# Attention with deferred value products: four key blocks at a time, and row maxima over two PSUM banks

## The chip, the cores and the metric

The kernel runs on one core of one Trainium2 chip, in one launch. The metric is the device time of that launch in microseconds (us). A core has a matrix engine (PE, with weight loads shown apart as PEld), a vector engine (DVE), an activation engine (ACT), a general engine (POOL) and a queue of transfers (SP). [...]

## The reference

One decoder layer on 4096 tokens of width 1024: RMSNorm, one input projection, three token mixers (a gated MLP over chunks, a gated linear recurrence, and attention with a forget bias), one output projection, residual and a final RMSNorm. Only the attention is touched. It has 8 heads of 64 channels and is causal:

```python
c = jnp.cumsum(jnp.transpose(log_f, (0, 2, 1)), axis=-1)
for blk in range(seq // C_BLOCK):                       # 128 queries
    s = einsum('bhqd,bhkd->bhqk', qh[q0:q1], kh[:q1]) * scale
    s = s + c[q0:q1, None] - c[None, :q1]
    s = where(mask, s, -inf)
    p = softmax(s, axis=-1)
    o = einsum('bhqk,bhkd->bhqd', p, vh[:q1])
```

## The kernel before, in words

Phase 1 (projection and the two other mixers, with the operands of attention written to DRAM) lasts until about 1661 us of the profiled span, attention from about 1674 to 3159 us, the output projection from there to the end.

Attention works on *units*: a pair of heads `p` (four of them) and a block `Q` of 512 queries (eight), 32 units in all. It has two passes.

- The row-max pass (`rowmax`, `rm_product`) forms scores with queries on the partitions: one product `sm` of 128 queries by 512 keys (line L128), whose maximum over the keys DVE finds with one instruction (`mp<-sm`, L137). Where the keys reach past the queries (the last 512 keys of a unit, "diagonal"), L132 adds the mask and takes the maximum, with a second small instruction that reads the result. `rm_tail` gathers a unit's maxima, transposes them on PE (`mt`, L1166) and they become an extra row of the query operand.
- The second pass takes one *step* for each block of 128 keys, 4(Q+1) in a unit, 576 in all. In a step each of the two heads has two accumulating products with keys on the partitions (`st`, L1353 and L1356), then ACT takes the exponential into a tile `pt` (L1360). `do_pv` multiplies `pt` by the values (`pv`, L1238; plain float32, 64 columns wide, one head on either half of the array, and so two instructions each on PE), and adds `pt` into a running sum: DVE for head 0, POOL for head 1 (`acc`, L1247). A step's `do_pv` is issued in the next step, behind the first of that step's two row-max products. On the diagonal POOL zeroes the weights of later keys (L1365) and the widths shrink to 384, 256 and 128.
- `finish_unit` is a generator advanced once a step by `tick(fin)`: it loads the gate, multiplies the sums by ones on PE to get the denominators (`pl`, L1206), takes their reciprocal by Ln and Exp on ACT (L1210, L1211) with a Newton step on DVE and POOL (L1213 to L1216), and scales `pv` (L1218).

The order of PE's instructions is the order of the code. On DVE, ACT and POOL the framework sets a fixed order when it builds the program. The row-max pass runs ahead by `LEAD` = 76 products, 38 steps; so the last 38 steps have no `sm`. PSUM in attention: two banks for `st` (pool `ps_st`), four for the tag `sm` (pool `ps_sm`: `sm`, `mt`, `pl`, and the output projection's `o`), two for `pv`. Tiles of a pool are given out in turn, and the next user of a buffer waits for the last reader of the one before.

Of the kernel before, what the change touches and what calls it, by code (L numbers as in the profile page):

```python
# [21 lines left out]
P = 128  # L22
# [11 lines left out]
def tile_trunk(  # L34
# [42 lines left out]
    # units of attention whose row maxima are found before the last projections  # L77
# [13 lines left out]
    def rsqrt_small(pool, ssum, n, scale, tag, y=None):  # L91
        """[P, n] sums -> 1/sqrt(sum * scale + EPS), full float32 accuracy."""
# [29 lines left out]

    def rm_product(ps, qb, kb, hi_, diag, tri, dst):
        """scores of 128 queries and 512 keys of one head, and their row maxima"""
# [13 lines left out]

    def rm_rows(p, Q, mp, mm, m2):
        """row maxima over all key groups, less the offset: high and low parts, negated"""  # L140
# [16 lines left out]
    # =====================================================================  # L157
    # Phase 1: RMSNorm, input projection, gMLP, HGRN2, FoX operands
    # =====================================================================
    with ExitStack() as p1:  # L160
# [68 lines left out]
        def xnorm(i0, n):  # L229
            """generator: reciprocal RMS of n token tiles from i0."""  # L230
# [8 lines left out]
        def xprep(T, own_norm=False):  # L239
            """generator: hT[T] = (hi, lo), [P, KC, 256] each."""  # L240
# [43 lines left out]
        def setup_gen():  # L284
            # gMLP
# [23 lines left out]
            # keep source position s (partition) <= target position t  # L309
# [7 lines left out]
            # softmax over the single layer, cumulative sum less its first row  # L317
# [17 lines left out]
            # mixing is linear: LayerNorm's gain goes after it, and its offset  # L335
            # becomes off[t, c] = ln_b[c] * sum_s w[t, s] + b_s[t]
# [6 lines left out]
            # masks of the levels inside a block of 32: [source s, targets in second halves]  # L343
# [7 lines left out]
            for li, h in enumerate(levels[2:]):  # L351
# [4 lines left out]
                # s - 2h*n >= 0  # L356
# [4 lines left out]
                # 2h*n + h - 1 - s >= 0  # L361
# [9 lines left out]
            # head selector columns  # L371
# [5 lines left out]
            # carried state, block-diagonal over the two heads of a tile  # L377
# [4 lines left out]
            # scores: zero for good where the source is in a later block than the target  # L382
# [13 lines left out]
        def hgrn(T):  # L396
            """generator for 256 tokens (two chunks), after its inputs are on chip."""
            z, qf, v = Zb.pop(T), Qf.pop(T), Vb[T]
            lb, oml = setup["lb"], setup["oml"]
            # sigmoid(z) = exp(-L), sigmoid(-z) = exp(-(z + L)), L = ln(1 + exp(-z))  # L400
# [28 lines left out]
            for st in range(len(levels) + 4):  # L429
                if st == 1:  # L430
                    dq = sm.tile([P, 8], F32, tag="dq", name="dq")
                    nc.vector.tensor_copy(dq, pd.rearrange("p c n -> p (c n)"))
                    sc = hg_state["sc"][0]  # r, (chunk, a), t
                    hg_state["sc"].rotate(-1)
                    # blocks of 32 on the diagonal, side by side
                    s32 = wk.tile([P, 8, 32], F32, tag="s32", name="s32", bufs=1)  # (chunk, a, r), t
# [6 lines left out]
                # take over the level scores  # L443
# [24 lines left out]
                # q / k times decay to the middle of each block  # L468
                li = st
                if 0 <= li < 7:  # L470
# [14 lines left out]
                    else:  # L485
                        # both heads' targets side by side, each over zeros in the other's rows
# [12 lines left out]
                if st == 7:  # L499
                    # carry terms  # L500
# [29 lines left out]
                # level products: the two heads of a tile go to different banks  # L530
# [87 lines left out]
            # RMS norm over the value channels  # L618
# [14 lines left out]
        def cgen(B):  # L633
# [12 lines left out]
            # log1p(e) = ln(u) + (e - (u - 1)) / u  # L646
# [43 lines left out]
            # reference offsets of each 512-query group, on all partitions  # L690
# [24 lines left out]
        def silu(ps, dst, scale=1.0):  # L715
            """dst = scale * silu(ps), scale a power of two; dst holds scale * ps meanwhile."""
# [7 lines left out]
        def gelu(ps, dst):  # L724
            """dst = gelu(ps), the tanh form written as x * sigmoid(2 y)."""
# [48 lines left out]
        def y_store(T, yt, row0, gain=1.0):  # L774
            """transpose token-major [P, 2, 256] and store at feature rows row0.."""
# [244 lines left out]
        for gi, (B, g) in enumerate(seq):  # L1020
# [6 lines left out]
            for ti in range(BT):  # L1027
# [10 lines left out]
                # next weights  # L1038
# [7 lines left out]
                # side work  # L1046
# [24 lines left out]
    # =====================================================================  # L1071
    # Phase 2: forgetting attention
    # =====================================================================
    nc.scalar.preload_act_table_set(LN_EXP_SET)
    with ExitStack() as p2:
        fs = p2.enter_context(tc.tile_pool(name="fs", bufs=3))
        ac = p2.enter_context(tc.tile_pool(name="ac", bufs=2))
        pp = p2.enter_context(tc.tile_pool(name="pp", bufs=7))
# [3 lines left out]
        ps_sm = p2.enter_context(tc.tile_pool(name="ps_sm", bufs=4, space=PSUM))  # L1082
# [22 lines left out]
        def load_ka(i):  # L1105
            """[k hi; k lo] and the values of 512 keys, two heads."""
# [21 lines left out]
        def rowmax():  # L1128
            """generator: each step is one score product of the row-max pass."""
            tails = []  # L1130
            for u, (p, Q) in list(enumerate(units))[U0:]:
# [5 lines left out]
                for cj in range(Q + 1):  # L1137
                    for hi_ in range(8):
                        ps = ps_sm.tile([P, 512], F32, tag="sm", name="sm")
                        rm_product(  # L1140
                            ps, qb, kb_t[p * NJ + cj], hi_, cj == Q, tri, mp[:, hi_, cj : cj + 1]
                        )
# [15 lines left out]
        def rm_tail(u, mp):  # L1158
# [4 lines left out]
            for _ in range(3 if u == 0 else 6):  # L1163
                yield
# [6 lines left out]
        def unit_load(u):  # L1171
            """query side of the second pass; the row maxima go below the low parts."""
# [23 lines left out]
        def finish_unit(u):  # L1196
            """generator: normalise, gate and store one unit's output."""
# [14 lines left out]
            # one Newton step: r (2 - l r)  # L1212
# [15 lines left out]
        def do_pv(u, kb, pts):  # L1228
            p, Q = units[u]
            nkb = 4 * (Q + 1)  # L1230
            q0, _ = q0_of(u, kb)
            if kb == 0:
# [97 lines left out]
        for si, (u, kb) in enumerate(steps):  # L1330
# [40 lines left out]
            if pend is not None:  # L1371
                do_pv(*pend)
# [119 lines left out]
```

## Time and profile before

| what | value |
|---|---|
| median of three timed runs | 3522.6 us (3509.25, 3522.6, 3523.05) |
| profiled execution, first to last instruction | 3516.6 us |
| attention in it | about 1674 to 3159 us |
| mean granted PE clock | 0.982 |
| busy: PE, DVE, ACT, POOL | 97%, 71%, 45%, 40% |

For the profiled execution the page gives its span alone, no time of its own; the span is 6.0 us below the median of the timed runs. In timeline rows the first number is the start and the second the duration in us, and xN merges N instructions that follow one another, their duration being that of the whole run. The end of a matrix product is modelled: successive products overlap, so that the distance between starts tells the rate. In rows of groups the numbers behind the count are total busy us and mean ns of one, then the engine's idle time ahead of them and what ended it. In rows of windows each engine's busy us stand with the number of instructions in brackets, then the granted clock (1.00 is full), the DMA share and GB/s.

### The profile page before, as it was taken

Reading aid. Unit: us, or ns where it says so; the run is one execution under the profiler, and the core shown is the slowest. Engines: PE = TensorE matmul, PEld = TensorE weight load, DVE = VectorE, ACT = ScalarE, POOL = GpSimd, SP = SyncE. Lnnn points to the kernel's source line nnn. Section 1 sums busy time; section 2 is a strip of 40 time slices with the busy share of each in tenths; the row PEclk is TensorE's granted clock in tenths of the full one; section 3 lists DMA queues with packets and bytes.
Section 4 is the critical chain, followed back from the end, with each engine's and each line's share of the span. In section 5 each row is a group of like instructions: output and inputs, shape, how many; then the busy total and the mean of one; then the engine's idle time right before and its main releaser. Section 6 shows DMA issues by size and latency. Waiting matters only on the chain.

```text
span 3516.6 us, 63564 instructions
## 1 busy us (share of the span) xinstructions
PE 3417.2 (97%) x24375; PEld 2569.8 (73%) x24375; DVE 2482.6 (71%) x5111; ACT 1584.4 (45%) x2883; POOL 1422.0 (40%) x1468
## 2 busy tenths in 40 slices
PE   7999999999999999988999999999999999999999
PEld 7999999999999998988444444444444444448887
DVE  6467746685467756782798878888889888965554
ACT  6335544356435543452345445454544554562221
POOL 2134422333134322352465466555665666570000
PEclk9999999999999999999799899999999999999999
DMA  5332333214332223212731141014101321013442
GB/s 178 109 94 64 97 127 116 79 53 159 97 104 68 70 85 111 67 49 78 155 77 34 49 118 43 19 41 120 55 28 28 97 64 37 28 64 135 148 146 96
DMA packets 227603, 297.75 MB, mean 85 GB/s; under 512 B 19602, under 2 KB 172448, under 8 KB 227298
## 3 DMA queue, kind: packets, MB, share of 16 engines
q1 hardware_dynamic: 227298, 293.69, 27.7%
q8 instruction: 191, 3.13, 0.4%
q14 instruction: 114, 0.93, 0.1%
HBM read 208.96 MB, written 84.43 MB: 83 GB/s over the span
## 4 chain that ended last, share of the span: by engine, by line
PE 76%; DVE 13%; ACT 4%; POOL 3%; issue 2%; DMA 2%; SPq 0%; DVEq 0%; POOLq 0%; ACTq 0%
PE acc L885 15%; PE pv L1238 13%; PE acc L906 12%; PE o L1430 10%; PE sm L128 9%; PE st L1353 7%; PE st L1356 6%; DVE wlo L211 2%; DVE acc L1247 1%; DMA x<-in_x_dram 1%; DVE mp L137 1%; PE pl L1206 1%; DVE gt L729 1%; DVE xq L494 1%; PE plb L557 1%
## 5 line engine op out<-in xcount | busy, mean ns | idle before, releaser
L1360 ACT ACTIVATE pt<-st,bias 128x512 f32<-128x512 f32 (+3 forms) x1152 | 692.0, 648 | 711.3 <-PE st L1356 699.3
L1247 POOL TENSOR_TENSOR acc<-acc,pt 128x512 f32<-128x512 f32 (+3 forms) x544 | 700.4, 1288 | 479.9 <-ACT pt L1360 469.4
L137 DVE TENSOR_REDUCE mp<-sm 128x1 f32<-128x512 f32 x896 | 590.1, 682 | 100.1 <-PE sm L128 92.3
L1238 PE MATMUL pv<-pt,v 128*64 128x512 f32 (+3 forms) x2304 | 587.7, 589 | 7.2 <-POOL pt L1365 4.5
L885 PE MATMUL acc<-hhi,whi 128*128 128x256 f32 x2048 | 580.7, 288 | 4.2 <-DVE q L718 2.3
L885 PE MATMUL acc<-hhi,wlo 128*128 128x256 f32 x2048 | 568.1, 282 | 0.0
L885 PE MATMUL acc<-hlo,whi 128*128 128x256 f32 x2048 | 567.3, 281 | 0.0
L906 PE MATMUL acc<-whi,hhi 128*128 128x256 f32 (+1 forms) x1792 | 518.3, 289 | 18.6 <-DVE gu L727 16.0
L1247 DVE TENSOR_TENSOR acc<-acc,pt 128x512 f32<-128x512 f32 (+3 forms) x544 | 506.5, 931 | 40.9 <-ACT pt L1360 30.4
L128 PEld LDWEIGHTS sm<-kb,qb 66*128 66x128 f32 x1152 | 218.1, 192 | 416.6 <-DVE mp L137 177.4
L906 PE MATMUL acc<-wlo,hhi 128*128 128x256 f32 (+1 forms) x1792 | 507.3, 283 | 0.0
L906 PE MATMUL acc<-whi,hlo 128*128 128x256 f32 (+1 forms) x1792 | 506.9, 283 | 0.0
L128 PE MATMUL sm<-kb,qb 66*128 66x512 f32 (+2 forms) x1152 | 494.2, 436 | 5.9 <-DVE mp L137 4.5
L1353 PE MATMUL st<-qa,ka 128*128 128x512 f32 (+2 forms) x1152 | 449.3, 392 | 12.4 <-DMA ka<-d_kl 12.4
L1356 PE MATMUL st<-qc,kb 68*128 68x512 f32 (+2 forms) x1152 | 442.3, 386 | 1.1 <-DMA qc<-d_m 1.1
L885 PEld LDWEIGHTS acc<-hhi,whi 128*128 128x128 f32 x2048 | 385.0, 190 | 7.8 <-DVE q L718 2.7
L885 PEld LDWEIGHTS acc<-hlo,whi 128*128 128x128 f32 x2048 | 384.2, 190 | 0.3 <-DVE hlo L273 0.2
L885 PEld LDWEIGHTS acc<-hhi,wlo 128*128 128x128 f32 x2048 | 384.3, 190 | 0.0
L906 PEld LDWEIGHTS acc<-whi,hhi 128*128 128x128 f32 x1792 | 341.9, 191 | 22.4 <-DVE gu L727 16.6
L906 PEld LDWEIGHTS acc<-wlo,hhi 128*128 128x128 f32 x1792 | 342.3, 191 | 0.1
L906 PEld LDWEIGHTS acc<-whi,hlo 128*128 128x128 f32 x1792 | 341.7, 191 | 0.0
L211 DVE SCALAR_TENSOR_TENSOR wlo<-wraw,gT,whi 128x256 fp32r<-128x256 f32 (+1 forms) x480 | 268.6, 600 | 58.1 <-ACT whi L210 56.8
(262 smaller groups left out, 4911.1 us busy)
## 6 DMA issues: line engine op xcount, KB each, us to landing
wraw<-in_w_in_dram SPq DMA_DIRECT2D x120, 512.0 KB
x<-in_x_dram SPq DMA_DIRECT2D x88, 512.0 KB
qa<-d_qh SPq DMA_DIRECT2D x64, 256.0 KB
out_dram<-x SPq DMA_DIRECT2D x31, 512.0 KB
kb<-d_kh SPq DMA_DIRECT2D x38, 256.0 KB
d_kh<-chi SPq DMA_DIRECT2D x32, 256.0 KB
d_kl<-clo SPq DMA_DIRECT2D x32, 256.0 KB
d_qh<-chi SPq DMA_DIRECT2D x32, 256.0 KB
```

The lines of the kernel that those rows point to most:

```text
L128: nc.tensor.matmul(ps[:, :n], qb[0:66, h, i * P : (i + 1) * P], kb[0:66, h, :n], start=True, stop=True)
L137: nc.vector.tensor_reduce(dst, ps[:, :use], axis=AX.X, op=ALU.max)
L211: nc.vector.scalar_tensor_tensor(lo[:, k, :n], raw, g, hi[:, k, :n].bitcast(F32), op0=ALU.mult, op1=ALU.subtract)
L494: nc.vector.tensor_tensor(xq[rows, :, r, :].rearrange("p g (n h) -> p g n h", h=h), sl(e), sl(qf), op=ALU.mult,)
L885: nc.tensor.matmul(ps[:, a, :], ww[:, k, cs], hh[:, k, :], start=n == 0, stop=n == 3 * KC - 1)
L906: nc.tensor.matmul(o, hh[:, k, ts_], ww[:, k, :width], start=n == 0, stop=n == 3 * KC - 1)
L1238: nc.tensor.matmul(pv[64 * h : 64 * h + 64, q0:], vt[:, kb % 4, 64 * h : 64 * h + 64], pts[h][:, q0:], start=kb == 0, stop=kb == nkb - 1,)
L1247: eng.tensor_tensor(a[:, q0:], a[:, q0:], pts[h][:, q0:], op=ALU.add)
L1353: nc.tensor.matmul(st[:, qm:], ka_t[g][:, h, cs], qa_t[u % 2][:, h, qm:], start=True, stop=False)
L1356: nc.tensor.matmul(st[:, qm:], kb_t[g][0:68, h, cs], qc_t[u % 2][:, h, qm:], start=False, stop=True)
L1360: nc.scalar.activation(pt[:, q0:], st[:, q0:], AF.Exp, bias=bias_of[u][:, h, kb : kb + 1])
L1430: nc.tensor.matmul(ps, a[:, k % 4, o : o + P], b[k][:, cs], start=n == 0, stop=n == 3 * KC - 1)
```

## The change

The matrix products are the same in number and shape. `do_pv` collects the `pt` of four steps (the four key blocks of 512 keys) and issues their 8 products (16 instructions on PE) together, in the first step of the next four. The sums move into `do_acc`, still one step late. `pp` grows from 7 to 13 tiles for this. The row-max pass takes two products a time into a tile of two banks, and one `tensor_reduce` over both gives two maxima (`rm_pair`; the diagonal keeps one instruction a product); `ps_sm` then holds two such tiles, of two banks each, in place of four of one bank, and `mt`, `pl` and `o` take such a tile too. A step issues one pair ahead of the value products, in place of one product ahead of them and one behind. The bookkeeping of key slots moves into `do_pv`. Line numbers shift: `st` L1367 and L1370, `pv` L1261, `acc` L1248, `sm` L147, its maximum L150, `pl` L1217, the reciprocal L1221, L1222 and L1224.

```diff
+    def rm_pair(ps, qb, kb, hi_, diag, tri, mp, cj):
+        if diag:
+            for n in range(2):
+                rm_product(ps[:, n, :], qb, kb, hi_ + n, True, tri, mp[:, hi_ + n, cj : cj + 1])
+            return
+        for n in range(2):
+            h, i = divmod(hi_ + n, 4)
+            nc.tensor.matmul(
+                ps[:, n, :], qb[0:66, h, i * P : (i + 1) * P], kb[0:66, h, :], start=True, stop=True
+            )
+        nc.vector.tensor_reduce(mp[:, hi_ : hi_ + 2, cj], ps, axis=AX.X, op=ALU.max)
...
-        pp = p2.enter_context(tc.tile_pool(name="pp", bufs=7))
+        pp = p2.enter_context(tc.tile_pool(name="pp", bufs=13))
...
-        ps_sm = p2.enter_context(tc.tile_pool(name="ps_sm", bufs=4, space=PSUM))
+        ps_sm = p2.enter_context(tc.tile_pool(name="ps_sm", bufs=2, space=PSUM))
...
-                    for hi_ in range(8):
-                        ps = ps_sm.tile([P, 512], F32, tag="sm", name="sm")
+                    for hi_ in range(0, 8, 2):
+                        ps = ps_sm.tile([P, 2, 512], F32, tag="sm", name="sm")
+                        rm_pair(ps, qb, kb_t[p * NJ + cj], hi_, cj == Q, tri, mp, cj)
...
+            for kb, pts in group:
+                q0, _ = q0_of(u, kb)
+                for h in (1, 0):
+                    nc.tensor.matmul(
+                        pv[64 * h : 64 * h + 64, q0:], vt[:, kb % 4, 64 * h : 64 * h + 64], pts[h][:, q0:],
...
+            group.append((kb, pts))
             rm_step()
-            if pend is not None:
-                do_pv(*pend)
-            pend = (u, kb, pts)
-            rm_step()
+            for h, pt in enumerate(late[2] if late else ()):
+                do_acc(late[0], late[1], h, pt)
+            late = (u, kb, pts)
             if rm_count[0] < 2 * si + LEAD:
                 rm_step()
+            if kb % 4 == 0 and pend is not None:
+                do_pv(*pend)
+                pend = None
+            if kb % 4 == 3:
+                pend, group = (u, kb // 4, group), []
             tick(fin)
```

How rows move. PE, in the middle of a unit, before (names: `qa`, `qc` queries, `kb` keys of the row-max pass and of the second product):

```order
L1353 MATMUL st<-qa_21725,ka 128x512
L1356 MATMUL st<-qc_21730,kb 128x512
L1353 MATMUL st<-qa_21725,ka 128x512
L1356 MATMUL st<-qc_21730,kb 128x512
L128 MATMUL sm<-kb,qb_21727 128x512
L1238 MATMUL pv<-pt,v 64x512 x2
L128 MATMUL sm<-kb,qb_21727 128x512
```

The same engine after the change, the last two steps ahead of a group of value products:

```order
L1367 MATMUL st<-qa_21725,ka 128x512
L1370 MATMUL st<-qc_21730,kb 128x512
L1367 MATMUL st<-qa_21725,ka 128x512
L1370 MATMUL st<-qc_21730,kb 128x512
L147 MATMUL sm<-kb,qb_21727 128x512 x2
L1367 MATMUL st<-qa_21725,ka 128x512
L1370 MATMUL st<-qc_21730,kb 128x512
L1367 MATMUL st<-qa_21725,ka 128x512
L1370 MATMUL st<-qc_21730,kb 128x512
L147 MATMUL sm<-kb,qb_21727 128x512 x2
L1261 MATMUL pv<-pt,v 64x512 x8
```

Three steps of four now consist of `st` and `sm` alone, and the value products of four follow in one run.

PE at the end of a unit, where the denominators `pl` are formed, before:

```order
L1238 MATMUL pv<-pt,v 64x512 x2
L128 MATMUL sm<-kb,qb_21727 128x512
L1206 MATMUL pl<-acc_25531,ones_v 64x512
L1206 MATMUL pl<-acc_25530,ones_v 64x512
L1353 MATMUL st<-qa_21725,ka 128x512
L1356 MATMUL st<-qc_21730,kb 128x512
L1353 MATMUL st<-qa_21725,ka 128x512
L1356 MATMUL st<-qc_21730,kb 128x512
L128 MATMUL sm<-kb,qb_21727 128x512
L1238 MATMUL pv<-pt,v 64x512 x2
L128 MATMUL sm<-kb,qb_21727 128x512
```

And after:

```order
L147 MATMUL sm<-kb,qb_21727 128x512 x2
L1217 MATMUL pl<-acc_25227,ones_v 64x512
L1217 MATMUL pl<-acc_25226,ones_v 64x512
L1367 MATMUL st<-qa_21725,ka 128x512
L1370 MATMUL st<-qc_21730,kb 128x512
L1367 MATMUL st<-qa_21725,ka 128x512
L1370 MATMUL st<-qc_21730,kb 128x512
L147 MATMUL sm<-kb,qb_21727 128x512 x2
L1367 MATMUL st<-qa_21725,ka 128x512
L1370 MATMUL st<-qc_21730,kb 128x512
L1367 MATMUL st<-qa_21725,ka 128x512
L1370 MATMUL st<-qc_21730,kb 128x512
```

No value products stand any more between `pl` and the second pair behind it, which takes `pl`'s buffer.

DVE in the same stretch (`acc` the sums, `rt` the Newton step and the scaled output, `mp` the maxima), before:

```order
L1247 TENSOR_TENSOR acc_25815<-acc_25815,pt 128x512
L137 TENSOR_REDUCE mp<-sm 128x1
L1213 TENSOR_TENSOR rt<-pl,rc 128x512
L137 TENSOR_REDUCE mp<-sm 128x1
L1214 TENSOR_SCALAR rt<-rt 128x512
```

And after, from the maximum of the pair that stands ahead of `pl`:

```order
L150 TENSOR_REDUCE mp<-sm 128x2
L1248 TENSOR_TENSOR acc_25491<-acc_25491,pt 128x512
L150 TENSOR_REDUCE mp<-sm 128x2
L1224 TENSOR_TENSOR rt<-pl,rc 128x512
L150 TENSOR_REDUCE mp<-sm 128x2
L1225 TENSOR_SCALAR rt<-rt 128x512
L150 TENSOR_REDUCE mp<-sm 128x2
L1248 TENSOR_TENSOR acc_25491<-acc_25491,pt 128x512
L1229 TENSOR_TENSOR rt<-pv,rc 128x512
L1248 TENSOR_TENSOR acc_25491<-acc_25491,pt 128x512 x2
L150 TENSOR_REDUCE mp<-sm 128x2 x3
```

DVE's last read of `pl` (L1224) stands behind a sum and the maximum of a whole pair; in the middle of a unit three maxima follow one another, and three of four sums stand together.

More of the change, by code (lines that the diff above doesn't have):

```diff
@@ L1137, in rowmax @@
                 for cj in range(Q + 1):
-                    for hi_ in range(8):
-                        ps = ps_sm.tile([P, 512], F32, tag="sm", name="sm")
-                        rm_product(
-                            ps, qb, kb_t[p * NJ + cj], hi_, cj == Q, tri, mp[:, hi_, cj : cj + 1]
-                        )
+                    for hi_ in range(0, 8, 2):
+                        ps = ps_sm.tile([P, 2, 512], F32, tag="sm", name="sm")
+                        rm_pair(ps, qb, kb_t[p * NJ + cj], hi_, cj == Q, tri, mp, cj)
                         yield
@@ L1162, in rm_tail @@
             rm_rows(p, Q, mp, mm, m2)
-            for _ in range(3 if u == 0 else 6):
+            for _ in range(2 if u == 0 else 3):
                 yield
@@ L1226, in tile_trunk, with do_acc, do_pv @@
         fin = []
-        def do_pv(u, kb, pts):
+        def do_acc(u, kb, h, pt):
+            q0, _ = q0_of(u, kb)
+            if kb == 0 and h == 0:
+                acc_of[u] = [ac.tile([P, 512], F32, tag=f"acc{i}", name=f"acc{i}") for i in range(2)]
+            eng, a = (nc.vector, nc.gpsimd)[h], acc_of[u][h]
+            if kb == 0:
+                eng.tensor_copy(a, pt)
+            else:
+                eng.tensor_tensor(a[:, q0:], a[:, q0:], pt[:, q0:], op=ALU.add)
+        def do_pv(u, j, group):
             p, Q = units[u]
             nkb = 4 * (Q + 1)
-            q0, _ = q0_of(u, kb)
-            if kb == 0:
+            if j == 0:
                 pv_of[u] = ps_pv.tile([P, 512], F32, tag="pv", name="pv")
-                acc_of[u] = [ac.tile([P, 512], F32, tag=f"acc{h}", name=f"acc{h}") for h in range(2)]
             pv = pv_of[u]
-            vt = v_t[p * NJ + kb // 4]
-            for h in (1, 0):
-                nc.tensor.matmul(
-                    pv[64 * h : 64 * h + 64, q0:], vt[:, kb % 4, 64 * h : 64 * h + 64], pts[h][:, q0:],
-                    start=kb == 0, stop=kb == nkb - 1,
-                )
-            for h, eng in ((0, nc.vector), (1, nc.gpsimd)):
-                a = acc_of[u][h]
-                if kb == 0:
-                    eng.tensor_copy(a, pts[h])
-                else:
-                    eng.tensor_tensor(a[:, q0:], a[:, q0:], pts[h][:, q0:], op=ALU.add)
-            if kb == nkb - 1:
+            vt = v_t[p * NJ + j]
+            for kb, pts in group:
+                q0, _ = q0_of(u, kb)
+                for h in (1, 0):
+                    nc.tensor.matmul(
+                        pv[64 * h : 64 * h + 64, q0:], vt[:, kb % 4, 64 * h : 64 * h + 64], pts[h][:, q0:],
+                        start=kb == 0, stop=kb == nkb - 1,
+                    )
+            if j == Q:
                 fin.append(finish_unit(u))
+            if Q == NJ - 1:
+                slots[0] += 2
+                vslots[0] += 1
         wo_hi, wo_lo = [], []
@@ L1304, in rm_step @@
                 next(rm)
-                rm_count[0] += 1
+                rm_count[0] += 2
             except StopIteration:
@@ L1328, in tile_trunk @@
             rm_step()
-        pend = None
+        pend, late, group = None, None, []
         for si, (u, kb) in enumerate(steps):
@@ L1333, in tile_trunk @@
             g = p * NJ + kb // 4
-            if Q == NJ - 1 and kb % 4 == 0 and kb > 0:
-                slots[0] += 2
-                vslots[0] += 1
-            if Q == 0 and kb == 0 and p > 0:
-                slots[0] += 2
-                vslots[0] += 1
             while g not in ka_t:
@@ L1382, in tile_trunk @@
                 unit_bias(u + 1)
+        for h, pt in enumerate(late[2]):
+            do_acc(late[0], late[1], h, pt)
         do_pv(*pend)
```

## The prediction

> **What bounds the kernel now.** I read the page's totals, then the windows of attention, PE's waits, and the timeline of a step.
>
> ```profile
> PE 3417.2 (97%) x24375; PEld 2569.8 (73%) x24375; DVE 2482.6 (71%) x5111; ACT 1584.4 (45%) x2883; POOL 1422.0 (40%) x1468
> PE 76%; DVE 13%; ACT 4%; POOL 3%; issue 2%; DMA 2%; SPq 0%; DVEq 0%; POOLq 0%; ACTq 0%
> 1673.66:3158.85 1485.19, 1469.42 (x5870) 716.05 (x5870) 1248.30 (x2159) 737.33 (x1226) 894.76 (x924) 0.98 0.23 62
> PE sm L128 <- DVE mp L137: 4.5, 7, 0.7
> PE pv L1238 <- POOL pt L1365: 4.5, 5, 1.7
> ```
>
> The first two rows say that PE is busy nearly always and carries the chain. The third is attention: PE busy 1469 of 1485 us, DVE 1248, ACT 737. The waits show that PE hardly waited for anyone there. What a change gains here is therefore PE time, and what it loses is waits that PE doesn't have now. One step in the middle of a unit:
>
> ```profile
> 2508.89 1.08 PE L1238 MATMUL pv<-pt,v 128*64 128x512 f32 x4
> 2509.90 0.50 PE L128 MATMUL sm<-kb,qb 66*128 66x512 f32 x1
> 2510.24 0.40 PE L1353 MATMUL st<-qa,ka 128*128 128x512 f32 x1
> 2510.47 0.40 PE L1356 MATMUL st<-qc,kb 68*128 68x512 f32 x1
> 2510.71 0.40 PE L1353 MATMUL st<-qa,ka 128*128 128x512 f32 x1
> 2510.95 0.40 PE L1356 MATMUL st<-qc,kb 68*128 68x512 f32 x1
> 2511.19 0.39 PE L128 MATMUL sm<-kb,qb 66*128 66x512 f32 x1
> 2511.51 0.65 PE L1238 MATMUL pv<-pt,v 128*64 128x512 f32 x2
> ```
>
> From `pv` to `pv` a step is 2.62 us. The full-width products start 0.235 apart. The one ahead of `pv` takes 0.32 to 0.33 (0.095 more) and the one behind it 0.34 (0.105 more: its weights weren't loaded ahead). So each excursion to the half-width products costs 0.20 us outside them.
>
> **Gain: fewer excursions.** Inside `pv` there is a cost as well. Once in the trace `pv` and `pl`, of one shape, follow each other directly:
>
> ```profile
> 3089.21 1.08 PE L1238 MATMUL pv<-pt,v 128*64 128x512 f32 x4
> 3090.12 1.03 PE L1206 MATMUL pl<-acc,ones_v 128*64 128x512 f32 x4
> 3091.08 0.50 PE L1353 MATMUL st<-qa,ka 128*128 128x512 f32 x1
> ```
>
> Eight instructions take 1.87 us, four take 1.01 (2508.89 to 2509.90). Four more in a run thus cost 0.86, and 0.15 of each `pv` is entry and exit. An excursion costs 0.20 + 0.15 = 0.35 us. A group of four has one in place of four: 1.05 us saved of 4 x 2.62 = 10.46. There are 144 groups (4 x 36), 112 of full width. [...]
>
> **Loss: the exponentials.** Without `pv`, PE comes back to a score buffer after 6 x 0.235 = 1.40 us, not 2.62. Can ACT follow?
>
> ```profile
> L1360 ACT ACTIVATE pt<-st,bias 128x512 f32<-128x512 f32 x960 | 608.9, 684 | 595.9 <-PE st L1356 587.0 <-DVE mp L137 7.0
> 2510.91 1.27 ACT L1360 ACTIVATE pt<-st,bias 128x512 f32<-128x512 f32 x2 [1.35 <-PE st L1356]
> 3087.23 1.27 ACT L1360 ACTIVATE pt<-st,bias 128x512 f32<-128x512 f32 x2 [0.96 <-PE st L1356]
> 3088.55 0.19 PEld L1353 LDWEIGHTS st<-qa,ka 128*128 128x128 f32 x1 [0.28 <-ACT pt L1360]
> 3088.55 0.50 PE L1353 MATMUL st<-qa,ka 128*128 128x512 f32 x1
> 3088.89 0.39 PE L1356 MATMUL st<-qc,kb 68*128 68x512 f32 x1
> ```
>
> An exponential starts 0.67 after its first score product (2510.24 to 2510.91), takes 0.684, and the second starts 0.59 behind the first (1.27 less 0.684). The last four rows are a case in which PE does wait: the exponentials end at 3088.50, the weight load comes at 3088.55, and the product takes 0.34 again. So PE resumes 0.05 + 0.105 = 0.16 behind ACT. Take the steps after a group of values, with time 0 at the first product; nothing is pending. Exponentials start at 0.67 and 1.25. Step 2: head 0 wants 1.40, may at 0.67 + 0.68 + 0.16 = 1.51; head 1 then wants 1.975, may at 1.25 + 0.84 = 2.09. Step 3: head 0 at 3.03 on time, head 1 at 3.60 in place of 3.50. Step 4: head 0 at 4.54 on time, head 1 at 5.12 in place of 5.00. Four waits, 0.45 us a group. It hides nowhere, since PE's order is fixed. On the diagonal (384, 256, 256 wide) the same working gives 0.5. The ends: 0, if the score weights may be loaded during the wait and ACT is a little quicker, and 0.8, if each of seven later products waits 0.11.
>
> Without `sm`, in the last 38 steps (8 full groups, about 1.5 diagonal), the working gives 9.36 us a group. A step there is now 2.16:
>
> ```profile
> 3103.99 0.50 PE L1353 MATMUL st<-qa,ka 128*128 128x512 f32 x1
> 3106.15 0.50 PE L1353 MATMUL st<-qa,ka 128*128 128x512 f32 x1
> ```
>
> That is 8.64 for four, so the end loses 0.7 x 8 + 1 = 7 us.
>
> **DVE and POOL.**
>
> ```profile
> L137 DVE TENSOR_REDUCE mp<-sm 128x1 f32<-128x512 f32 x896 | 590.1, 682 | 100.1 <-PE sm L128 92.3
> L1247 DVE TENSOR_TENSOR acc<-acc,pt 128x512 f32<-128x512 f32 x448 | 457.0, 1020 | 33.7 <-ACT pt L1360 30.4 <-POOL pt L1365 1.8
> L1247 POOL TENSOR_TENSOR acc<-acc,pt 128x512 f32<-128x512 f32 x448 | 623.4, 1392 | 474.4 <-ACT pt L1360 469.4
> L1406 DVE TENSOR_TENSOR ylo<-yr,yhi 128x1024 fp32r<-128x1024 f32 x32 | 40.5, 1265 | 43.0 <-ACT yhi L1405 42.2 <-PE st L1353 0.8
> ```
>
> A maximum over two banks isn't in the trace. Bounds: 1.36 (two of 0.682) and 1.07 (twice 0.682 less a fixed part of up to 0.3); 1024 elements elsewhere take 1.265. I take 1.2. DVE then has 4 x 1.2 + 4 x 1.02 = 8.9 us in a group of 9.85, POOL 5.6. Three maxima run at 1.2 a step against PE's 1.4 to 1.55, and three sums fall under the 3.6 us of `pv`, so that in mid-unit DVE keeps up; 436 pairs save about 70 us of DVE, which is not on the path.
>
> **Loss: the end of a unit.** `pl` takes one of now two `sm` buffers, and the second pair behind it waits until DVE has read it (L1213, now L1224).
>
> ```profile
> 2503.89 1.08 PE L1206 MATMUL pl<-acc,ones_v 128*64 128x512 f32 x4
> 2505.02 0.60 ACT L1210 ACTIVATE rc<-pl 128x512 f32<-128x512 f32 x1 [1.89 <-PE pl L1206]
> 2506.83 0.63 ACT L1211 ACTIVATE rc<-rc 128x512 f32<-128x512 f32 x1
> 2508.44 0.68 DVE L1213 TENSOR_TENSOR rt<-pl,rc 128x512 f32<-128x512 f32 x1
> ```
>
> Now that takes 5.2 us from 2503.89, and two steps with `pv` cover it. After: step 1 ends at 1.40, `pl` starts at 1.50, its successor at 2.61; Ln 2.63 to 3.23; exponentials of step 2 from 3.28 and 3.87; Exp until 5.1. DVE's order is: sum of step 2 (its weights come at 3.96; until 4.68), maximum of pair 2 (until 5.88), L1224 (until 6.5). PE reaches pair 3 at 5.22 and gets the buffer at 6.66: 1.44 us lost. With the two score waits on the way, step 4 ends 1.38 later than a group plus the 1.09 that `pl` cost before (1.01 as for four `pv` instructions, and a slower neighbour). About three of 32 units end beside no `sm`, so 29 x 1.38 = 40 us. Ends: 0.6 a unit, if pair 2's maximum hides, and 2, if POOL delays the sum.
>
> `mt` takes a buffer too, and then the pair behind it waits for the maximum just issued; that is there already:
>
> ```profile
> 2197.13 0.28 PE L1166 MATMUL mt<-ident,m 128*16 128x128 f32 x1
> 2198.08 0.50 PE L128 MATMUL sm<-kb,qb 66*128 66x512 f32 x1 [0.68 <-DVE mp L137]
> ```
>
> With pairs of 1.2 I put 0.35 more on each of 29 units (bounds 0 and 1.2), and 0.3 for the diagonal's maxima beside bunched sums: 19 us. SP's rows and the slots move by a step and load far ahead: nothing.
>
> **Sum.** 104 full groups x (1.05 - 0.45) = 62; 30 diagonal x 0.55 = 16; less 40, 19 and 7: 12 us gained. The profiled 3516.6 becomes about 3505, and the median, 6 higher, 3510.
>
> **Rivals.** *Small waits.* If `pl` is read early, unit ends cost as before and only score waits remain: 62 + 16 - 7 = 71, 3452 us. Without those either, 104 x 1.05 + 30 x 1.05 = 141 less 7: 3390. Against it speaks DVE's order, fixed as shown; for it, that my latencies add up in series.
>
> *The clock halves at unit ends*, which ends slower.
>
> ```profile
> 1716.21:1719.62 3.41, 2.26 (x10) 1.04 (x9) 3.41 (x12) 0.51 (x2) 1.17 (x4) 1.00 1.05 225
> 1719.62:1726.45 6.83, 6.83 (x20) 3.55 (x19) 4.54 (x9) 2.75 (x4) 1.51 (x2) 0.50 1.08 231
> 1972.21:1975.62 3.41, 1.88 (x9) 0.68 (x5) 3.41 (x10) 0.42 (x1) 2.05 (x3) 1.00 0.00 0
> 1975.62:1996.10 20.48, 20.48 (x55) 10.57 (x57) 11.50 (x30) 5.59 (x10) 5.99 (x12) 0.50 0.22 53
> 2828.95:2832.36 3.41, 2.51 (x14) 1.27 (x12) 2.36 (x4) 2.04 (x4) 3.27 (x6) 1.00 0.33 104
> 2832.36:2835.77 3.41, 3.41 (x19) 1.80 (x18) 3.41 (x7) 1.48 (x4) 3.30 (x6) 1.00 0.13 50
> ```
>
> After 3.41 us with 1.15 or 1.53 us of idle PE the clock was half for 7 or 20 us; after 0.90 it stayed. The wait at `pl` gives 1.15 idle (1.44 less 0.11 of load and the 0.17 by which a product's modelled end overlaps the next): just there. A drop costs half its length, 4 us where a dense `pv` group follows; at half of 29 units, 58 us: 3568. It decides from a wait of about 1.4 us upward. [...]
>
> *DVE becomes the bound*, where sums wait for POOL (1020 ns mean against 680 alone): at 1.4 a sum and 1.36 a maximum a group takes 11.0, over 10.46: 104 x 0.55 = 57 us slower, less what the diagonal saves, about 3560. *The two-bank maximum saves nothing* (1.36): unit ends grow by 0.2, 3516.
>
> **Chances.** As summed 0.43 (own range 3492 to 3535); small waits 0.27; clock 0.20; DVE 0.10. Differences within 0.5% (3505 to 3540) are no change that this kernel's measurement can tell. Faster: small waits and a third of the first, 0.41; slower: clock, most of DVE, 0.29; same 0.30. Leaving the extremes out, the range is 3430 to 3570.
>
> **What would show it.** A run of 16 `pv` instructions should take 3.59 us to the next product; steps of `st` and `sm` alone 1.5 us; a two-bank maximum 1.2; PE should wait for ACT at `st`, some 0.1 at a time, and for L1224 at `sm` by 1.4 at each unit's end, with PE's idle in attention risen from 16 us to about 60 (29 x 1.15 on top of what there is, and a few at `mt`). I am wrong if PE's waits for DVE stay few, if the exponentials don't hold PE, or if the clock is below 0.97.

## The result, and the profile after

The changed kernel takes 3682.07 us (median of 4 runs, 3669.73 to 3696.92) against 3515.93 for the kernel before on the same chip (four timed runs; the table above has three of them): ratio 1.0485, 95% interval 1.0462 to 1.0507. It is 166 us slower where 12 us faster was forecast, and lies outside the range of 3430 to 3570. The profiled execution has a span of 3681.9 us and a mean granted clock of 0.956.

From the page and the views of the changed kernel: the totals, the window of attention, PE's waits, and the group of the new maximum.

```profile
PE 3464.0 (94%) x24375; PEld 2628.7 (71%) x24375; DVE 2378.8 (65%) x4675; ACT 1603.4 (44%) x2883; POOL 1402.0 (38%) x1468
1673.33:3326.60 1653.27, 1519.47 (x5877) 777.88 (x5878) 1145.14 (x1724) 757.80 (x1228) 874.77 (x924) 0.92 0.21 56
PE sm L128 <- DVE mp L132: 88.4, 114, 2.1
PE sm L147 <- DVE mp L150: 26.0, 42, 0.9
PE st L1367 <- ACT pt L1374: 7.3, 24, 0.8
L150 DVE TENSOR_REDUCE mp<-sm 128x2 f32<-128x1024 f32 x436 | 524.8, 1219 | 35.0 <-PE sm L147 34.2
```

Attention lasts 1653 us in place of 1485, and so the whole loss is there. PE's idle in it is 1653.27 - 1519.47 = 134 us (before 16, and about 60 were forecast), and its clock is 0.92 (before 0.98). DVE has *less* to do than before, 65% of the span, so it is no bound by amount. The third row is the new one: PE waits 114 times, 88.4 us in all, at L128, the products of the diagonal, for DVE's masked maximum. These are not the waits that were forecast (for `pl`, and for ACT: of the latter the view shows 7.3 us, the rest lies in the length of the steps, below). One such place, the end of the row-max pass of a unit, PE and DVE in order of time, some rows left out:

```profile
2498.69 0.28 PE L128 MATMUL sm<-kb,qb 66*128 66x256 f32 x1
2498.93 1.10 DVE L1248 TENSOR_TENSOR acc<-acc,pt 128x512 f32<-128x512 f32 x1
2499.95 0.28 DVE L132 CUSTOM_DVE_ANT_0 sm<-sm,tri 128x128 f32<-128x128 f32 x1
2500.35 0.58 PE L128 MATMUL sm<-kb,qb 66*128 66x256 f32 x1 [1.37 <-DVE mp L132]
2500.86 5.03 PE L1261 MATMUL pv<-pt,v 128*64 128x512 f32 x16
...
2506.63 0.34 PE L128 MATMUL sm<-kb,qb 66*128 66x384 f32 x1
2507.00 0.57 DVE L132 CUSTOM_DVE_ANT_0 sm<-sm,tri 128x384 f32<-128x384 f32 x1 [4.36 <-PE sm L128]
2507.68 0.50 PE L128 MATMUL sm<-kb,qb 66*128 66x512 f32 x1 [0.72 <-DVE mp L132]
2508.50 0.29 PE L128 MATMUL sm<-kb,qb 66*128 66x256 f32 x1
2509.28 0.39 PE L128 MATMUL sm<-kb,qb 66*128 66x256 f32 x1 [0.50 <-DVE mp L132]
2509.99 0.34 PE L128 MATMUL sm<-kb,qb 66*128 66x384 f32 x1
2511.05 0.80 PE L128 MATMUL sm<-kb,qb 66*128 66x512 f32 x1 [0.72 <-DVE mp L132]
```

In each of the four pairs the first product is issued, DVE masks it and takes its maximum, and only then does PE issue the second product. `rm_pair` calls `rm_product` twice there, product, maximum, product, maximum, into one tile of two banks. Before the change each product had a bank and a buffer of its own, and PE ran on. PE's wait for L132 in attention before, and the first pair of a diagonal there, some rows left out:

```profile
PE sm L128 <- DVE mp L132: 0.9, 1, 0.9
2484.20 0.28 PE L128 MATMUL sm<-kb,qb 66*128 66x256 f32 x1
2485.43 0.39 PE L128 MATMUL sm<-kb,qb 66*128 66x256 f32 x1
2486.49 0.29 DVE L132 CUSTOM_DVE_ANT_0 sm<-sm,tri 128x128 f32<-128x128 f32 x1
```

The second product starts 1.06 us ahead of the masked maximum of the first. In the changed kernel's first pair a sum stands ahead of the masked maximum on DVE as well, and PE waits 1.37 us.

What follows such a wait stands in the windows of the same stretch, cut where the clock changes; behind each engine's busy us the granted clock is the first of the last three numbers:

```profile
2496.84:2500.26 3.42, 2.13 (x9) 1.23 (x7) 3.06 (x6) 2.59 (x4) 3.13 (x4) 1.00 0.44 106
2500.26:2503.67 3.41, 3.32 (x9) 1.25 (x11) 2.39 (x5) 0.00 (x0) 1.75 (x2) 0.50 0.45 132
2503.67:2507.08 3.41, 3.29 (x17) 1.29 (x13) 0.08 (x1) 0.60 (x2) 0.00 (x0) 1.00 0.01 4
2507.08:2510.50 3.42, 2.15 (x12) 1.63 (x12) 2.91 (x11) 1.84 (x5) 3.03 (x6) 1.00 0.24 72
2510.50:2513.91 3.41, 2.86 (x7) 2.15 (x7) 2.22 (x9) 1.07 (x3) 1.55 (x6) 0.50 0.71 178
2513.91:2517.32 3.41, 3.41 (x10) 1.01 (x10) 1.56 (x2) 0.42 (x1) 0.90 (x2) 0.50 0.49 139
2517.32:2520.73 3.41, 3.41 (x22) 1.88 (x19) 0.99 (x2) 1.18 (x3) 1.06 (x3) 1.00 0.00 0
```

After a window with 1.27 to 1.29 us of idle PE the clock is half for one or two windows. The 16 value instructions at 2500.86 then take 5.03 us, where the same run elsewhere takes 3.65. Summed from the trace's clock records, attention has 257 us at half clock, before it had 56. Of these, 21 and 29 us belong to a stretch that began ahead of attention's first product; the rest are 41 stretches now, and before two, together 27 us, besides a last one cut off by attention's end. At a granted clock of 0.50 a stretch costs, by my estimate, at most half its length; half of 257 - 56 is up to 100 us more. The other 68 us of attention's 168 are then waits, less what the grouping gains.

The 41 windows of 3.41 us ahead of these stretches hold 0.61 to 1.85 us of idle PE, 34 of them more than 1.00. The longest idle is at the diagonal (L128, for L132) in 29, at a pair behind a unit's end in 7, elsewhere in 5. Of the 367 full-clock windows that full clock followed none holds more than 1.00, but 49 hold 0.61 or more, so that this trace gives no sharp limit.

### The profile page after: what moved, and what is told of

Read it like the earlier page. It is cut to its first block, busy times and chain, and to the rows that moved or that the text cites. A ratio compares the mean times of both kernels' runs of the same rounds, so it can differ in the third digit from the quotient of the medians.

```text
span 3681.9 us, 63074 instructions
## 1 busy us (share of the span) xinstructions
PE 3464.0 (94%) x24375; PEld 2628.7 (71%) x24375; DVE 2378.8 (65%) x4675; ACT 1603.4 (44%) x2883; POOL 1402.0 (38%) x1468
## 4 chain that ended last, share of the span: by engine, by line
PE 70%; DVE 16%; ACT 5%; issue 4%; POOL 3%; DMA 2%; SPq 0%; DVEq 0%; POOLq 0%; ACTq 0%
PE acc L898 15%; PE pv L1261 13%; PE acc L919 10%; PE o L1453 9%; PE st L1367 7%; PE sm L147 5%; PE st L1370 5%; DVE mp L150 3%; DVE acc L1248 2%; PE sm L128 2%; DVE wlo L224 2%; ACT pt L1374 2%; DMA x<-in_x_dram 1%; PE pl L1217 1%; DVE gt L742 1%
## 5 line engine op out<-in xcount | busy, mean ns | idle before, releaser
L1374 ACT ACTIVATE pt<-st,bias 128x512 f32<-128x512 f32 (+3 forms) x1152 | 713.2, 650 | 892.3 <-PE st L1370 878.3
L1248 POOL TENSOR_TENSOR acc<-acc,pt 128x512 f32<-128x512 f32 (+3 forms) x544 | 679.1, 1248 | 602.4 <-ACT pt L1374 593.7
L1248 DVE TENSOR_TENSOR acc<-acc,pt 128x512 f32<-128x512 f32 (+3 forms) x544 | 438.1, 805 | 255.7 <-ACT pt L1374 174.7
L1261 PE MATMUL pv<-pt,v 128*64 128x512 f32 (+3 forms) x2304 | 558.6, 633 | 0.8 <-POOL pt L1379 0.8
L150 DVE TENSOR_REDUCE mp<-sm 128x2 f32<-128x1024 f32 x436 | 524.8, 1219 | 35.0 <-PE sm L147 34.2
L1367 PE MATMUL st<-qa,ka 128*128 128x512 f32 (+2 forms) x1152 | 507.7, 441 | 21.4 <-DMA ka<-d_kl 13.2
L1370 PE MATMUL st<-qc,kb 68*128 68x512 f32 (+2 forms) x1152 | 450.6, 392 | 0.0
L1367 PEld LDWEIGHTS st<-qa,ka 128*128 128x128 f32 x1152 | 222.5, 193 | 287.7 <-ACT pt L1374 148.1
L1261 PEld LDWEIGHTS pv<-pt,v 128*64 128x64 f32 x2304 | 170.6, 153 | 335.4 <-issue 307.9
L147 PE MATMUL sm<-kb,qb 66*128 66x512 f32 x872 | 297.6, 426 | 29.6 <-DVE mp L150 26.0
```

The costliest lines, as they stand in the source:

```text
L147: nc.tensor.matmul(ps[:, n, :], qb[0:66, h, i * P : (i + 1) * P], kb[0:66, h, :], start=True, stop=True)
L150: nc.vector.tensor_reduce(mp[:, hi_ : hi_ + 2, cj], ps, axis=AX.X, op=ALU.max)
L1248: eng.tensor_tensor(a[:, q0:], a[:, q0:], pt[:, q0:], op=ALU.add)
L1261: nc.tensor.matmul(pv[64 * h : 64 * h + 64, q0:], vt[:, kb % 4, 64 * h : 64 * h + 64], pts[h][:, q0:], start=kb == 0, stop=kb == nkb - 1,)
L1367: nc.tensor.matmul(st[:, qm:], ka_t[g][:, h, cs], qa_t[u % 2][:, h, qm:], start=True, stop=False)
L1370: nc.tensor.matmul(st[:, qm:], kb_t[g][0:68, h, cs], qc_t[u % 2][:, h, qm:], start=False, stop=True)
```

## The experiments

Each run has a median, a ratio to the kernel before on the same chip with its 95% interval, and from its profiled execution PE's waits for row maxima (all rows of `sm` waiting for `mp`, summed) and the time at half clock between the first score product and the last value product, from the clock records. The kernel before was run again with each set: 3508.3 us beside e1 to e4, 3510.3 beside e5 to e8, 3513.5 beside e9 to e11, 3514.7 beside e12. So differences of a few us between rows of different sets are better read from the ratios. Waits and half clock are of one execution each; e7's is the slowest of its four, 13 us above the median.

| kernel | us | ratio | waits for maxima | half clock |
|---|---|---|---|---|
| before | 3515.9 | 1 | 5 | 56 |
| after | 3682.1 | 1.0485 (1.0462 to 1.0507) | 117 | 257 |
| e1: after, both diagonal products first | 3538.7 | 1.0083 (1.0060 to 1.0107) | 48 | 93 |
| e2: grouped values, single maxima | 3606.7 | 1.0273 (1.0254 to 1.0293) | 69 | 205 |
| e3: pairs, values in each step | 3681.8 | 1.0482 (1.0457 to 1.0508) | 85 | 209 |
| e4: e2, three `st`, three `sm` buffers | 3620.1 | 1.0313 (1.0292 to 1.0334) | 102 | 295 |
| e5: e2, late unit end | 3533.3 | 1.0056 (1.0036 to 1.0076) | 34 | 110 |
| e6: e1, late unit end | 3537.5 | 1.0065 (1.0046 to 1.0085) | 43 | 103 |
| e7: e3, both diagonal products first | 3544.2 | 1.0087 (1.0054 to 1.0120) | 18 | 118 |
| e8: e4, late unit end | 3581.0 | 1.0187 (1.0159 to 1.0215) | 82 | 243 |
| e9: e5, unit end on DVE | 3498.1 | 0.9961 (0.9950 to 0.9973) | 14 | 93 |
| e10: e8, unit end on DVE | 3484.6 | 0.9923 (0.9908 to 0.9938) | 26 | 113 |
| e11: before, late unit end on DVE | 3516.3 | 1.0008 (0.9995 to 1.0022) | 4 | 56 |
| e12: e6, unit end on DVE | 3504.8 | 0.9977 (0.9961 to 0.9992) | 29 | 76 |

**The order inside a diagonal pair (e1).** The only edit, in part (`...` stands for lines left out):

```diff
         if diag:
+            uses = []
             for n in range(2):
-                rm_product(ps[:, n, :], qb, kb, hi_ + n, True, tri, mp[:, hi_ + n, cj : cj + 1])
...
+                nc.tensor.matmul(
+                    ps[:, n, :w], qb[0:66, h, i * P : (i + 1) * P], kb[0:66, h, :w], start=True, stop=True
+                )
+            for n, use in enumerate(uses):
+                nc.vector.tensor_tensor_reduce(
...
             return
```

> The changed kernel, but on the diagonal both products of a pair are issued before the two masked maxima, so that the second product does not stand behind DVE's work on the first half of its tile. Theory A (the in-pair wait, 114 times and 88 us in the changed kernel's trace, and the clock halvings it sets off, are the loss): PE's waits for L132 fall below 10 us, the half-clock time in attention falls from about 266 us to under 110, and the time to 3470 to 3510. Rival B (short idle at unit ends and at st sets off the halvings, whatever the diagonal does): half-clock time stays above 180 us and the time is about 3590.

```profile
PE sm L159 <- DVE mp L162: 35.2, 57, 0.9
PE sm L148 <- DVE mp L152: 6.7, 11, 1.5
```

L148 and L152 are the diagonal's product and maximum here. Their waits fall from 88.4 us to 6.7, the half clock from 257 us to 93, and 143 of the 166 us come back. The cause of most of the loss is thereby shown: the turn of PE and DVE inside one tile, with the clock that it costs. What stays is 29 us above the kernel before (by the ratio), with 35 us of waits between ordinary pairs; my range of 3470 to 3510 missed that.

**Each half of the change alone (e2, e3).** e3 keeps `do_pv` as before and takes only the pairs. e2 keeps `do_pv` grouped and takes single maxima in four buffers of one bank:

```diff
-        ps_sm = p2.enter_context(tc.tile_pool(name="ps_sm", bufs=2, space=PSUM))
+        ps_sm = p2.enter_context(tc.tile_pool(name="ps_sm", bufs=4, space=PSUM))
...
+                    for hi_ in range(8):
+                        ps = ps_sm.tile([P, 512], F32, tag="sm", name="sm")
+                        rm_product(ps, qb, kb_t[p * NJ + cj], hi_, cj == Q, tri, mp[:, hi_, cj : cj + 1])
...
             rm_step()
+            rm_step()
```

> Only the pairs: two products a time into two banks, one maximum for both, diagonal as in the changed kernel; value products each step as before. Theory A: the 116 in-pair waits are there with 0.8 us each, and set off halvings: 90 us of waits and some 60 to 90 us by the clock, 3640 to 3700. Rival B: 3500 to 3540, since no steps without value products exist.

> Only the deferred value products: row maxima one product a time in four single banks, both products of a step ahead of the values. Theory A: no pair, no in-pair wait; the groups save 0.5 us each as in the changed kernel's plain groups (9.97 against 10.46), unit ends give some back: 3480 to 3510. Rival B (the deferral itself is what costs, by waits for ACT and by the clock): 3560 or more.

```profile
PE sm L128 <- DVE mp L132: 83.3, 116, 3.3
PE sm L128 <- DVE mp L137: 60.8, 28, 3.7
```

The first row is of e3, the second of e2. The pairs alone lose what the whole change loses, 3681.8 against 3682.1, as theory A said for e3. But grouping alone loses too, 98 us against the kernel before in the same set, and that I had not expected. Rival B of e2 named such a time, but its waits for ACT come to 8 us here; what the trace shows are 28 waits for maxima of up to 3.7 us, about one a unit. One of them, in e2, from the timeline:

```profile
2256.20 0.69 DVE L1231 TENSOR_TENSOR rt<-pv,rc 128x512 f32<-128x512 f32 x1 [1.80 <-POOL rc L1229]
2257.14 1.28 POOL L1250 TENSOR_TENSOR acc<-acc,pt 128x512 f32<-128x512 f32 x1 [0.96 <-ACT pt L1376]
2257.41 4.91 DVE L1250 TENSOR_TENSOR acc<-acc,pt 128x512 f32<-128x512 f32 x3
2258.71 1.39 POOL L1250 TENSOR_TENSOR acc<-acc,pt 128x512 f32<-128x512 f32 x1 [0.29 <-ACT pt L1376]
2260.28 1.49 POOL L1250 TENSOR_TENSOR acc<-acc,pt 128x512 f32<-128x512 f32 x1 [0.18 <-ACT pt L1376]
2262.24 3.67 DVE L137 TENSOR_REDUCE mp<-sm 128x1 f32<-128x512 f32 x6
2262.97 1.40 PE L128 MATMUL sm<-kb,qb 66*128 66x512 f32 x2 [3.62 <-DVE mp L137]
2264.16 0.63 PE L1369 MATMUL st<-qa,ka 128*128 128x512 f32 x1
```

DVE stands still for 1.80 us, most of it behind the value products (these end at about 2255), since the last step of a unit's end (L1231) waits for POOL's second multiplication of `rc`. Then three sums take 4.91 us, 1.64 each, in turn with POOL's sums of 1.3 to 1.5; alone one takes 0.69 (the changed kernel, while POOL waits):

```profile
2473.98 0.69 DVE L1248 TENSOR_TENSOR acc<-acc,pt 128x512 f32<-128x512 f32 x1 [3.00 <-ACT pt L1374]
```

Six maxima are queued behind the slow sums in e2, and PE waits 3.62 us. Behind it a score product takes 0.63 in place of 0.50 and the clock is 0.50 (2262.82 to 2266.20). Two things are mixed here, the wait for POOL and the slow sums. The changed kernel and e1 have the same wait for POOL (56 and 55 us in all, e2 55) but there PE waits for no ordinary pair longer than 0.9 us; why single maxima suffer more from it than pairs was not tested.

**Three score buffers (e4).** e2 with `ps_st` of three and `ps_sm` of three buffers.

> The deferral alone, with three score buffers and three single banks for the row-max products in place of two and four. Theory: the waits of st for the exponentials (0.45 us a group by the working, 0.5 by the plain group's 9.97) go, since a score buffer returns after one and a half steps: plain groups of 9.4 to 9.5 us, and 40 to 60 us less than the deferral with two score buffers, 3430 to 3460. Rival: three sm banks bring the waits back at sm, and the time equals that of the deferral with two score buffers.

It missed: 3620.1. The waits for maxima rose from 69 to 102 us, as the rival said, which fits the bank taken from them; the edit changes both pools at once, so that this was not shown apart. The same edit pays only once most of these waits are gone (e10).

**The unit's end later (e5, e6, e8).** In each the last product of `finish_unit` is moved two steps on:

```diff
             nc.gpsimd.tensor_tensor(r, r, zt, op=ALU.mult)
             yield
+            yield
+            yield
             nc.vector.tensor_tensor(t, pv, r, op=ALU.mult)
```

> The kernel with grouped values and single maxima (3606.7), with the last step of a unit's end (the product of the values and rc on DVE, which waits for two multiplications on POOL) moved two steps later; nothing else. In that kernel the wait of DVE for POOL's rc (54.5 us, 29 times) stands ahead of three sums and six maxima, and then PE waits 3.62 us for a maximum, once a unit, and the clock is halved for 6.8 us behind it. Theory C: that wait is what makes the maxima late. Then the waits of PE for maxima fall from 69 us to under 20, the time at half clock in attention from 205 us to under 110, and the time is 3606.7 - 29 x 2.8 - 50 = about 3475 (3450 to 3500), under the kernel before. Rival D: DVE is late because its sums and POOL's slow each other (three sums in 4.9 us), and waits for POOL only pass time that it would lose anyway: PE's waits stay over 45 us and the time is 3570 to 3620.

> The kernel of pairs whose two diagonal products are both issued ahead of their maxima (3538.7), with the same move of the unit's last product by two steps. Theory C: the waits for pairs' maxima (42 us) fall under 25 and the half clock from 93 us to about 60: 3500 to 3525. Rival D: the waits come from two buffers of pairs with slow sums between, and stay over 35 us: 3530 to 3545.

> Grouped values, single maxima in three banks, three score buffers (3620.1), with the unit's last product two steps later. Theory C: waits for maxima fall from 102 us to under 40 and half clock from 295 to under 130: 3620 - 29 x 2.6 - 80 = about 3465, 3440 to 3500, about as much as with two score buffers or up to 28 us less. Rival D: waits stay over 70 us, 3590 or more.

e5 gains 73 us on e2, which lost 98, and DVE's waits for POOL's `rc` fall from 54.5 us to 9.8, so that these waits were most of e2's loss. But it comes to 3533, not under 3500: both theories were partly right. e6 gains 1 us, where rival D held. e8 gains 39 us, and its waits stay at 82; its 3581 lies between what theory and rival gave. In e5 the same place reads:

```profile
2290.15 3.40 DVE L1252 TENSOR_TENSOR acc<-acc,pt 128x512 f32<-128x512 f32 x2
2293.47 3.67 DVE L137 TENSOR_REDUCE mp<-sm 128x1 f32<-128x512 f32 x6
2294.20 1.22 PE L128 MATMUL sm<-kb,qb 66*128 66x512 f32 x2 [1.95 <-DVE mp L137]
```

The wait for POOL is gone, the slow sums (1.70 each) are not, and PE still waits 1.95.

**Pairs without the turn and without grouping (e7).** e3 with the edit of e1.

> Values in each step as before, row maxima in pairs, both diagonal products of a pair ahead of their maxima; against the same kernel with the products in turn (3681.8). Theory A: the product that waits for DVE inside its own pair is the whole loss of pairs: PE's waits at the diagonal fall from 83 us to under 35, the half clock from 209 us to under 100, and the time to 3510 to 3545. Rival E: two maxima of a diagonal pair behind one another hold the next pair as long, and only half of the loss goes: over 3580.

3544.2, at the edge of what theory A said: 138 of e3's 174 us (3681.8 against 3508.3) come back by the order of two products and two maxima. The waits fall to 18 us but the half clock only to 118, above the 100 expected. Of the 118, 32 us began ahead of attention. The other 86 are nine stretches of 3.4 to 20.5 us, each behind a window with 1.19 to 1.92 us of idle PE in one to three waits; three of the nine come with a wait of the value products, which the table's column leaves out.

**The unit's end on DVE (e9, e10, e12, and e11 as the control).** POOL's two multiplications go to DVE, two steps later, behind the value products of the fifth step of the next unit. Against e5, where the last product was two steps late, it now comes one step sooner:

```diff
-            nc.gpsimd.tensor_tensor(r, r, t, op=ALU.mult)
-            nc.gpsimd.tensor_tensor(r, r, zt, op=ALU.mult)
-            yield
             yield
             yield
+            nc.vector.tensor_tensor(r, r, t, op=ALU.mult)
+            nc.vector.tensor_tensor(r, r, zt, op=ALU.mult)
             nc.vector.tensor_tensor(t, pv, r, op=ALU.mult)
```

> Grouped values, single maxima, unit's last step two steps later (3533.3), with the two multiplications of rc moved from POOL to DVE, behind the values of the unit's fifth step; nothing else. In that kernel, in the unit's second group, POOL is late by its two multiplications, and its sums then run beside DVE's: these take 1.7 us each where alone they take 0.68 (2290.15: two in 3.40), six maxima are queued behind, and PE waits 1.95. Theory F: without those multiplications POOL's sums come early and DVE's take 0.7 to 1.0 there; PE's waits for maxima fall from 33 us to under 12, the half clock in attention from 110 to under 75, and the time to 3533 - 29 x 1.7 - 20 = about 3465 (3445 to 3490), under the kernel before. Rival G: DVE is merely too full (three products more of 0.68 on it) and is late anyway: waits stay over 25 us, time 3520 to 3560.

> The same move of the two multiplications, in the kernel with three score buffers and three buffers of single maxima (3581.0). Theory F: waits for maxima from 82 us to under 35, half clock from 243 us to under 130: about 3480 (3440 to 3510). Rival G: with one maximum's buffer fewer DVE is late anyway, waits over 60, over 3550.

> The kernel before with the same late end of a unit on DVE; values in each step, single maxima, nothing grouped: the control for the one above. PE waits for maxima 4.5 us in all there, so under both theories nothing is to be had: 3500 to 3520. Should it gain 20 us or more, the gain of the run above isn't the grouping's.

> The changed kernel mended as far as the runs before allow: pairs, both diagonal products ahead of their maxima, and the unit's end late and its two multiplications on DVE (3537.5 with them on POOL). The waits for pairs left there are two a unit: 0.54 us where pl holds a buffer (2487 and its like), and 0.81 in the group behind, where DVE's sums run beside a late POOL. Theory F: the second goes, 29 x 0.8 = 23, and some of the half clock: 3500 to 3520, no faster than the same with single maxima (3498.1). Rival H: with two buffers any sum of 0.7 us more in DVE's row holds a pair: the three products more on DVE take back what POOL gives, 3530 to 3545.

```profile
PE sm L128 <- DVE mp L137: 14.1, 20, 0.9
PE sm L128 <- DVE mp L137: 23.4, 45, 1.8
PE sm L159 <- DVE mp L162: 20.6, 41, 0.9
```

These are e9, e10 and e12. e9 gains 35 us on e5 and is the first to beat the kernel before, by 0.4%; 3465 was too much to expect, and 3498.1 lies above the range given. At the place shown for e5 a wait of 0.93 is left, and a sum there still takes 1.78 beside POOL, so that only a part of the slow sums went. e10 gains 96 us on e8 and is the fastest, 3484.6, ratio 0.9923: with the long waits gone, the third score buffer pays (3498.1 without it, e9). The control e11 moves nothing (3516.3), so the gains of e9 and e10 are not the move's alone: it pays only where the values are grouped. e12, the changed kernel with the pair mended and the end on DVE, comes to 3504.8, as theory F said; the two-bank maximum gains nothing over single maxima (e9, 3498.1).

In all, e10's attention, by its window:

```profile
1672.96:3120.20 1447.24, 1405.27 (x5873) 777.43 (x5874) 1221.68 (x2221) 728.92 (x1228) 813.71 (x862) 0.96 0.24 64
```

That is 38 us under the 1485 of the kernel before, in single executions (the medians differ by 29), with 42 us of PE still idle and a clock of 0.96 against 0.98. Of its 113 us at half clock 17.5 began ahead of attention. The rest are 16 stretches behind windows with 0.47 to 2.20 us of idle PE, nine of them with a wait for a maximum of 0.8 to 0.9 us.

## Why the prediction was wrong, point by point

**Fewer excursions, and the exponentials: right for a plain group.** A full group with nothing pending, from the changed kernel, PE's first score product of each step and the values:

```profile
2472.48 0.51 PE L1367 MATMUL st<-qa,ka 128*128 128x512 f32 x1
...
2482.92 0.50 PE L1367 MATMUL st<-qa,ka 128*128 128x512 f32 x1
2484.43 0.50 PE L1367 MATMUL st<-qa,ka 128*128 128x512 f32 x1
2486.05 0.41 PE L1367 MATMUL st<-qa,ka 128*128 128x512 f32 x1
2487.62 0.40 PE L1367 MATMUL st<-qa,ka 128*128 128x512 f32 x1
2489.29 3.65 PE L1261 MATMUL pv<-pt,v 128*64 128x512 f32 x16
2492.88 0.50 PE L1367 MATMUL st<-qa,ka 128*128 128x512 f32 x1
```

The 16 value instructions take 3.59 us to the next product, as forecast. The first step takes 1.51 as worked out, the next two 1.62 and 1.57; the whole group 9.96 in place of 9.85. A plain group thus saves 0.50 of 10.46 and not 0.60. But only 18 of the 143 distances from one run of values to the next lie between 9.9 and 10.0. The others hold something more or less (an `mt`, a unit's end, a wait, the diagonal), so that no row shows the 62 us summed for 104 groups. In the last steps without `sm` I reckoned with 9.36; the trace has 9.49.

**The two-bank maximum: right.** 1.219 us against 1.2. The fixed part of up to 0.3 in its lower bound was an estimate: two single maxima of 0.682 are 0.145 longer than one of two banks, and a whole masked maximum over 128 keys takes 0.29 (L132 at 2486.49, above).

**`mt`: near in size, not in kind.** The group before, 2472.48 to 2482.92, holds an `mt` and takes 10.44, which is 0.48 more, for 0.35 forecast. But the pair behind that `mt` starts 0.38 after it, and no row shows it waiting for a maximum; how much of the 0.48 the kernel before paid as well was not measured.

**The end of a unit: too large, and another wait.** Of the 1.44 us at the second pair behind `pl`, 0.55 is there. In 10 units 0.80 more comes 10.9 us later, in the next group, where DVE's sums run beside POOL's (two in 2.44 us from 2291.47, beside POOL's at 2292.09 and 2293.66). From the timeline of the changed kernel:

```profile
2284.11 0.68 DVE L1224 TENSOR_TENSOR rt<-pl,rc 128x512 f32<-128x512 f32 x1
2284.24 0.73 PE L147 MATMUL sm<-kb,qb 66*128 66x512 f32 x2 [0.55 <-DVE mp L150]
2295.11 0.73 PE L147 MATMUL sm<-kb,qb 66*128 66x512 f32 x2 [0.80 <-DVE mp L150]
```

The pair at 2284.24 starts while DVE still reads `pl` (L1224 ends at 2284.79), and its row names the maximum of the pair before. So it doesn't take `pl`'s buffer, as the section on the change and the working had it: it takes the other one, and the read of `pl` is a wait of PE only once in attention, for 0.3 us. All waits of ordinary pairs for ordinary maxima come to 26 us, where 40 were put down for the ends of units.

**The diagonal: the step that failed.** "0.3 for the diagonal's maxima" a unit, 9 us in all, saw the diagonal as a matter of DVE's load. The waits measure 88.4 us, 3.0 for each of 29 units, and the change itself made them: in the quoted diff two calls of `rm_product` fill one tile. The rows of order ahead of the prediction are of mid-unit and of the unit's end; the diagonal, where the turn stands, is not among them.

**The clock: halvings behind idle PE right, place and size wrong.** The rival put halvings at unit ends, at 58 us and 0.20. The unit's end has its halvings too, 7 of the 41: three behind a window with about 1.14 us of idle PE (waits of 0.26 and 0.88), as the rival worked out, others behind a wait of 0.5 to 0.8. But 29 come with the waits of the diagonal, and all together they cost up to 100 us. The limit that I took, 1.15 us halving and 0.90 not, was too sharp: 0.61 was enough once. The rival took 4 us for a drop; the 41 stretches are 3.41, 6.83 or 10.24 us long (20, 14 and 7 of them), of which half is 1.7, 3.4 or 5.1. The two misses, 88 - 9 = 79 and 100, are 179 us, about the 178 between the 12 gained and the 166 lost. That they meet so closely is partly luck: the 100 is an upper bound, and the misses of the other terms are left out. Shown by experiment is that the waits at the diagonal, and most of the added half clock, go when the order inside the pair is changed (e1).

**DVE as the bound: no by amount, yes by order.** It has less work than before, but its order is fixed, and PE waited for what stood behind a sum or a wait for POOL (3.62 us in e2, 1.95 in e5, 0.93 in e9, at the places shown). The sign I gave for being wrong, a clock below 0.97, came true: 0.956.

What stays open: why the same idle halves the clock in one window and not in another, and why a stretch at half clock can last longer where the values stand in each step (up to 27 us in e3, 20.5 in e7 and before) than in the grouped kernels (at most 13.7).

## What to carry to other kernels

Before two products share a tile, read each branch that fills it: if a reader of the first half is issued ahead of the writer of the second, the two engines take turns (here 114 waits of 88.4 us in all, 6.7 us with both products first, e1). Price a wait of PE with the clock behind it: by the sums above, 117 us of waits came with up to 100 us lost by the clock. And where long products that hid the other engines' work are gathered into one place, the steps left bare depend on the queues of those engines: what stands there must be moved behind the long products too (e9, 35 us under e5), or a gain of 0.5 us a group doesn't show (e2, 98 us above the kernel before).

## What the runs showed of the hardware

That waits of some tenths of a microsecond add up to a halved clock again and again was not expected: 41 times in attention, where before it was two or three times, and behind windows of 3.41 us with 0.61 to 1.85 us of idle PE. That length is the trace's own: every stretch of the clock records, full or half, lasts a multiple of 3.41 us, but for the last of each trace (7.0 us before, 6.1 after).

In the rows shown a sum of two operands on DVE takes 0.69 us alone and 1.64 to 1.70 on average while POOL runs sums of its own. Of the 448 sums of 128x512 in the changed kernel's trace, the 85 that no instruction of POOL overlaps take 0.67 to 0.69; the other 363 take 0.67 to 1.79, 0.91 on average. So a sum beside POOL can be slow and need not be; what decides it was not shown.
